# Sums of squares in four column groups, bonus sums in two float32r passes, block copies on GpSimd

## The chip, the cores and the metric

The kernel runs on one core of a Trainium2 chip. The metric is the time of one execution on the device, in microseconds (us). The core's engines work side by side, each through its own instructions in a fixed order: TensorE (PE; PEld is its loading of weights), VectorE (DVE), ScalarE (ACT), GpSimd (POOL) and SyncE (SP), which issues most of the DMAs.

## The reference

One inference step of a decoder with two layers, on a prompt of 256 tokens and eight tokens of eight running sequences, 264 columns in all. The model width is 1024, the inner width of the feed-forward blocks 2816. Each layer is a half-weighted SwiGLU, a mixer and another half-weighted SwiGLU, each behind an RMSNorm. The mixer of layer 0 is RWKV-7 time mixing with 16 heads of 64 channels, that of layer 1 is retention. The change lies in the first of these:

```python
r = xr @ wr;  k = xk @ wk;  v = xv @ wv
kk = hd(k * k_k)
kk = kk / jnp.maximum(jnp.sqrt(jnp.sum(kk * kk, axis=-1, keepdims=True)), 1e-12)
...
def step(S, inp):
    r_t, d_t, k_t, v_t, kk_t, a_t = inp
    sa = jnp.einsum('bhvk,bhk->bhv', S, -kk_t)
    S = (S * d_t[:, :, None, :] + sa[..., None] * (kk_t * a_t)[:, :, None, :]
         + v_t[..., None] * k_t[:, :, None, :])
    return S, jnp.einsum('bhvk,bhk->bhv', S, r_t)
...
y = y + jnp.sum(r_h * k_h * r_k.astype(f32), axis=-1, keepdims=True) * v_h
```

The sum of `kk * kk` over the 64 channels of each head is called the sums of squares below, and the sum in the last line the bonus.

## The kernel before

**Matrices.** The channels lie on the partitions in eight tiles of 128, so every activation is a 128x264 tile; a tile of 128 channels holds two heads, a pair. The weights come as 128x128 blocks, eight to a unit of 512 KB, which SyncE loads into one of three buffers (`raw`). Most products are done in float32r, in three passes over parts of the operands: ScalarE copies the unit to `hi` (`split`), VectorE subtracts it to give `lo`, and the matmuls are `ah,hi`, `al,hi` and `ah,lo`. The products for r, k and v in the time mixing (`xr,raw`, `xk,raw`, `xv,raw`) read the float32 block as it is, and float32 matmuls appear as two records each.

**Order.** The weight products are one main stream. Everything else of the layer is written as generators that stand beside it, each with a rank (`beside`). `weave` decides at each step of the stream which of them goes on, by modelled costs of every operation (`spent`) and by marks that one sets and another waits for (`mark`, and `yield` of a mark's name). From that program a scheduler fixes the order on every engine, in which its instructions then run one after another. So a change of any operation can move others that it doesn't touch.

**Time mixing.** These generators matter here.

- `lengths(g, sqs)`, for two groups of four pairs: matmuls with `hsel`, a 128x16 selection for each pair, add the squares of all four pairs into 16 rows of one PSUM tile; then square root, maximum and reciprocal give `rnr`.
- `stage(f)`, for each pair f: a matmul with `selT`, a 16x128 selection, brings the two rows of the pair back onto 128 partitions.
- `inverse`: a substitution of 32 steps on VectorE inverts the triangular blocks of all chunks; it ends with the mark `W0`. VectorE transposes the result (`AT`), ScalarE copies it into the blocks of `X` (L811 and on), and TensorE makes `tm,AT` and `V,AT` from it.
- `prep(f)`: the bonus operand `rc`, the product of r, k and `r_k`; for pairs 4 to 7 it begins behind the mark `W0`, for pairs 0 to 3 before it, but the last product, which gives `s_["bon"]`, comes behind `W0` for all.
- `heads2(p)`, for two pairs of tiles at a time: TensorE makes `KQ`, `PI,ka`, `cst,vt`, `VK,KQ`, `z,X` and others; ScalarE brings results from PSUM to SBUF (`bT`, `aT`, `vt`, `VK`, `z`). It ends with the bonus, a float32 matmul of `rc` with `bones`, a 128x128 constant with ones where two channels have the same head, shown as `ps<-rc,cst`.
- `decode`: the eight single tokens, with their states (`dS`, 512 KB each) loaded on GpSimd's queue and multiplied as `dS,kkr`.

The constants (`cst`, 128x1412) come by one DMA on ScalarE's queue, `selT` by another. A selection that is 32 wide, `rows64`, and its counterpart `back` are among the constants before too; the output norm uses them.

Of the kernel before, what the change touches and what calls it, by code (L numbers as in the profile page):

```python
# [11 lines left out]
F32R = mybir.dt.float32r  # L12
# [29 lines left out]
class Step:  # L42
# [158 lines left out]
    def mark(self, key):  # L201
        self.done[key] = self.now
# [242 lines left out]
class Rwkv(Step):  # L445
    def rw_consts(self, p):

        nc = self.nc
        c = p.tile([128, NCST], F32, name="cst")
        nc.scalar.dma_start(c, self.io["cst"])  # L450
        self.ident = c[:, CST["ident"]:CST["ident"] + 128]
        self.bones = c[:, CST["bones"]:CST["bones"] + 128]
        self.hsel = c[:, CST["hsel"]:CST["hsel"] + 128].rearrange("p (f h) -> p f h", f=KT)
        col = lambda k, n: c[:, CST[k]:CST[k] + n]
        self.m_ak, self.m_up = col("m_ak", 64), col("m_up", 64)
        self.m_kq = col("m_ak", 128)
        self.eye2 = col("eye2", 64)
        self.centre = col("centre", 128)
        self.rows64 = col("rows64", 64).rearrange("p (i m) -> p i m", i=2)
        self.back = col("back", 256).rearrange("p (i n) -> p i n", i=2)  # L460
        self.diag = col("diag", 4)
        self.pick = col("pick", 128).rearrange("p (e q n) -> p e q n", e=2, q=2)
        self.rst = col("rst", 256)

    def rwkv(self, gain):
# [6 lines left out]
        with ExitStack() as ctx:  # L472
# [19 lines left out]
                return h, l  # L492

            sh, xt = self.sh, self.xt

            hv = P1.tile([128, 4, KT], F32, name="hv")
            for i, k in enumerate(("w0", "a0", "ka")):
# [2 lines left out]
            epsg = P1.tile([128, 1], F32, name="epsg")  # L500
            nc.gpsimd.memset(epsg, 64e-5)
            big = lambda name: P.tile([128, 1024], F32, tag="big", name=name, bufs=3)
            selT = big("selT")[0:16].rearrange("p (f n) -> p f n", f=KT)
            nc.scalar.dma_start(selT, self.io["selT"])

            X = P1.tile([128, 32, 64], F32, name="X")
            for p0 in (32, 96):
# [200 lines left out]
            def lengths(g, sqs):  # L708
                yield f"k{g}"
                ssq = ps_()  # L710
                for j in range(4):
                    self.mm(ssq[0:16, 0:T], self.hsel[:, 4 * g + j, :], sqs[j], j == 0, j == 3)
                rn = tmp("mx")[0:16]
                self.act(rn, ssq[0:16, 0:T], AF.Sqrt)
                self.ts(rn, rn, 1e-12, None, ALU.max)
                rnr[g] = slot("rnr")[0:16]
                self.vec("reciprocal", rn, out=rnr[g])
                mark(f"rn{g}")
                yield
# [34 lines left out]
            def stage(f):  # L754
                yield f"rate{f}"
                yield f"rn{f // 4}"
                if f >= TU["SW"]:
                    yield "W0"
                if f >= 2:
                    yield f"stage{f - 2}"  # L760
                s_ = st[f]
                ta, cc, pp = s_["ta"], s_["cc"], s_["pp"]
                rb = ps_()[:, 0:T]
                self.mm(rb, selT[:, f, :], rnr[f // 4])
                kkn = tmp("kkn")
                self.stt(kkn, s_["k"], par("kk", f), rb)

                t_, kd = tmp("mx"), s_["k"]
                self.act(t_, ta, AF.Identity, scale=hv[:, 2, f:f + 1], bias=hv[:, 3, f:f + 1])
                self.tt(kd, t_, kd)  # L770
                u = ta
                self.stt(u, ta, 1.0, kkn, ALU.add, ALU.mult)
                gather(1, f, kkn[:, NP:T])
                nc.gpsimd.tensor_scalar(out=dq[:, 2, f, :], in0=u[:, NP:T], scalar1=-0.5, scalar2=None, op0=ALU.mult)
                gather(3, f, kd[:, NP:T])
                al, be, ka = (quarter(slot(n, 256)) for n in ("al", "be", "ka"))
                self.stt(al, r4(kkn), -1.0, pp[:, :, 0:64])
                self.stt(be, r4(u), 0.5, cc)
                self.tt(ka, r4(kd), cc)
                s_.update(rho=pp[:, :, 1:65], bon=kd, al=al, be=be, ka=ka)  # L780
                mark(f"stage{f}")
                yield

                pa = quarter(ps_()[:, 0:256])
                for c in range(NC):
                    for e0 in EH:
                        s, lo, hi = slice(e0, e0 + 64), slice(0, 32), slice(32, 64)
                        for r, i, j in ((lo, lo, 0), (hi, hi, 0), (hi, lo, 32)):
                            self.mm(pa[e0 + r.start:e0 + r.stop, c, j:j + 32], al[s, c, r], be[s, c, i])
                self.act(Ag[:, :, 4 * f:4 * f + 4].rearrange("p s n -> p n s"), pa[:, :, 0:32])  # L790
                for e0 in EH:
                    self.act(AT[e0 + 32:e0 + 64, 4 * f:4 * f + 4], pa[e0 + 32:e0 + 64, :, 32:64])
                mark(f"A{f}")
# [3 lines left out]
            def inverse():  # L797
                V, tm = (big(n).rearrange("p (a b) -> p a b", b=32) for n in ("V", "tm"))
                flat32 = lambda t: t.rearrange("p a b -> p (a b)")
                nc.gpsimd.memset(V, 0.0)  # L800
                nc.gpsimd.memset(flat32(V)[:, 0:1024:33], 1.0)
                for f in range(KT):
                    yield f"A{f}"
                self.turn(A3.rearrange("p r s -> p s r"), Ag)
                for m in range(31, 0, -1):
                    n = 32 - m
                    o = tm[:, 0:n, 0:m]
                    self.tt(o, V[:, m:32, m:m + 1].to_broadcast([128, n, m]),
                            A3[:, m:m + 1, 0:m].to_broadcast([128, n, m]))
                    self.tt(V[:, m:32, 0:m], V[:, m:32, 0:m], o, ALU.add)  # L810
                    if TU["INVY"] and m % TU["INVY"] == 0:  # L811
                        yield

                Xd = tm
                self.turn(Xd.rearrange("p n i -> p i n"), V)
                mark("W0")
                for e0 in EH:
                    self.turn(AT[e0:e0 + 32], Xd[e0:e0 + 32])
                for e0 in EH:
                    self.act(X[e0 + 32:e0 + 64, :, 32:64], Xd[e0 + 32:e0 + 64])  # L820
                    self.act(X[e0:e0 + 32, :, 0:32], Xd[e0:e0 + 32])
                yield
                for g in range(2):
                    py = ps_().rearrange("p (n s) -> p n s", n=16)
                    for n in range(16):
                        for e0 in EH:
                            hi = slice(e0 + 32, e0 + 64)
                            self.mm(py[e0:e0 + 32, n], AT[hi, 16 * g + n], Xd[hi, 16 * g + n])
                    for e0 in EH:
                        self.act(V[e0:e0 + 32, 16 * g:16 * g + 16], py[e0:e0 + 32])  # L830
                    yield
                for g in range(2):
                    px = ps_().rearrange("p (n s) -> p n s", n=16)
                    for n in range(16):
                        for e0 in EH:
                            lo = slice(e0, e0 + 32)
                            self.mm(px[lo, n], AT[lo, 16 * g + n], V[lo, 16 * g + n])
                    for e0 in EH:
                        self.act(X[e0:e0 + 32, 16 * g:16 * g + 16, 32:64], px[e0:e0 + 32])
                    mark(f"X{g}")  # L840
                    yield

            def prep(f):
# [8 lines left out]
                yield "W0"  # L852
                self.stt(rc, rc, par("rk", f), s_["bon"])
                s_["bon"] = rc
                mark(f"bon{f}")
                yield

# [10 lines left out]
            def heads2(p):  # L868
# [76 lines left out]
                for f, s_ in zip(fs, s2):  # L945
                    yield f"bon{f}"
                    pbo = ps_()[:, 0:T]
                    self.mm(pbo, self.bones, s_["bon"])
                    self.tt(s_["bon"], pbo, s_["vt"])
                yield  # L950
                pl = two()
# [193 lines left out]

CST = {}
_c = 0
for _k, _w in (("ident", 128), ("bones", 128), ("hsel", 128), ("m_ak", 64), ("m_up", 64), ("eye2", 64), ("centre", 128),
               ("rows64", 64), ("back", 256), ("diag", 4), ("pick", 128), ("rst", 256)):
    CST[_k] = _c  # L1150
    _c += _w
# [3 lines left out]
def consts():  # L1155
# [8 lines left out]

    put("ident", np.eye(128))
    put("bones", h[:, None] == h[None, :])
    hs = np.zeros((128, KT, 16))
    for f in range(KT):
        hs[p, f, 2 * f + h] = 1
    put("hsel", hs.reshape(128, 128))  # L1170

    put("m_ak", q[:, None] < s)
    put("m_up", q[:, None] <= s)
# [17 lines left out]
    r = np.ones((128, 4, 64))  # L1191
    r[:, :, 0] = 0
    put("rst", r.reshape(128, 256))
    sel = np.zeros((16, KT, 2, 64), np.float32)
    for f in range(KT):
        for e in range(2):
            sel[2 * f + e, f, e] = 1
    return c, sel.reshape(16, KT, 128)


def pack_wkv(s):
# [363 lines left out]

# [34 lines left out]
```

## Time and profile before

| | |
|---|---|
| median of three runs | 1288.61 us (1284.57 to 1290.11) |
| profiled execution | 1283.95 us, of which the span of the trace is 1282.2 |
| mean granted TensorE clock | 0.996 of full speed |
| TensorE busy | 1254.6 us, 98% |
| weight load, beside TensorE | 1184.4 us, 92% |
| VectorE, ScalarE, GpSimd busy | 849.4, 674.1, 68.8 us |

The span runs from the first to the last recorded instruction; the execution's time has 1.75 us more. Times inside the trace count from the start of the span. The time mixing lies between about 200 and 430 us and the retention's state sums at 869 us; feed-forward blocks stand around both. A row that covers several instructions has the start of the first and the time from there to the end of the last one; ends of matmuls are modelled.

### The profile page before, as it was taken

What the parts mean: (1) busy time and instruction counts of PE and PEld (TensorE: products, weight loads), DVE (VectorE), ACT (ScalarE), POOL (GpSimd) and SP (SyncE); (2) the same over time, 40 slices, a digit from 0 to 9 for tenths busy, and PEclk for the clock granted to TensorE, in tenths of its full rate; (3) what the DMA queues carried; (4) which work ended last, traced back from release to release, by engine and by line L of the source; (5) the groups of instructions that cost most, each with busy time, mean ns of one, the idle gap of its engine ahead of it and who ended that gap; (6) DMA issues with size and microseconds to landing.
All of it is one profiled execution on the core that took longest, in us unless ns stands there. A gap on an engine that the chain in (4) does not pass through costs nothing.

```text
span 1282.2 us, 29100 instructions
## 1 busy us (share of the span) xinstructions
PE 1254.6 (98%) x12194; PEld 1184.4 (92%) x12194; DVE 849.4 (66%) x1391; ACT 674.1 (53%) x1169; POOL 68.8 (5%) x175
## 2 busy tenths in 40 slices
PE   9999999999988999999999999999999999999996
PEld 9999998678777999999999999988888799999996
DVE  6766567589246877766566656677877865766554
ACT  7544442653444777754456454445665554544542
POOL 0000001131200000000000000011111100000000
PEclk9999999999999999999999999999999999999998
DMA  7655554333401566665557555679879655555562
GB/s 236 196 181 181 180 167 140 100 101 117 158 14 43 182 215 216 213 198 181 180 196 264 181 181 181 203 255 348 306 254 329 224 181 180 175 181 180 179 182 83
DMA packets 66755, 239.16 MB, mean 187 GB/s; under 512 B 7504, under 2 KB 8912, under 8 KB 66496
## 3 DMA queue, kind: packets, MB, share of 16 engines
q1 hardware_dynamic: 59472, 212.63, 51.8%
q0 software_dynamic: 6544, 23.40, 4.9%
q8 instruction: 95, 1.56, 0.5%
q10 hardware_dynamic: 608, 1.28, 0.3%
q14 instruction: 36, 0.29, 0.1%
HBM read 214.92 MB, written 22.35 MB: 185 GB/s over the span
## 4 chain that ended last, share of the span: by engine, by line
PE 87%; issue 5%; DMA 3%; DVE 2%; ACT 2%; SPq 0%; DVEq 0%; POOL 0%; ACTq 0%; POOLq 0%
PE ps L138 86%; DMA raw<-in_w 2%; PE ps L153 1%; DVE lo L105 1%; ACT hi L90 1%; DMA dS<-in_wkvt 1%; DMA Sd<-in_wkv 0%; DMA S<-in_ret 0%; ACT L90 0%; DMA out_swkv<-Sd 0%; DVE yl L105 0%; DVE xf L105 0%; DVE on L120 0%; DVE rs L126 0%; ACT sd L90 0%
## 5 line engine op out<-in xcount | busy, mean ns | idle before, releaser
L90 ACT ACTIVATE hi<-raw 128x1024 fp32r<-128x1024 f32 (+1 forms) x344 | 362.6, 1054 | 428.3 <-PE ps L138 210.4
L105 DVE TENSOR_TENSOR lo<-raw,hi 128x1024 fp32r<-128x1024 f32 (+1 forms) x344 | 418.5, 1217 | 229.6 <-ACT hi L90 228.1
L138 PE MATMUL ps<-ah,hi 128*128 128x264 f32 (+1 forms) x1824 | 522.0, 288 | 0.9 <-ACT ah L90 0.8
L138 PE MATMUL ps<-al,hi 128*128 128x264 f32 (+1 forms) x1824 | 515.8, 284 | 0.0
L138 PE MATMUL ps<-ah,lo 128*128 128x264 f32 (+1 forms) x1824 | 513.3, 284 | 0.1
L138 PEld LDWEIGHTS ps<-ah,hi 128*128 128x128 f32 x1824 | 342.0, 188 | 9.2 <-issue 7.4
L138 PEld LDWEIGHTS ps<-al,hi 128*128 128x128 f32 x1824 | 342.7, 188 | 4.1 <-issue 2.9
L138 PEld LDWEIGHTS ps<-ah,lo 128*128 128x128 f32 x1824 | 341.5, 188 | 0.5 <-DVE lo L105 0.3
L138 PE MATMUL ps<-hh,hi 128*128 128x264 f32 x832 | 237.1, 285 | 0.0
L138 PE MATMUL ps<-hl,hi 128*128 128x264 f32 x832 | 237.0, 285 | 0.0
L138 PE MATMUL ps<-hh,lo 128*128 128x264 f32 x832 | 236.8, 285 | 0.0
L138 PEld LDWEIGHTS ps<-hl,hi 128*128 128x128 f32 x832 | 156.8, 188 | 0.0
L138 PEld LDWEIGHTS ps<-hh,lo 128*128 128x128 f32 x832 | 156.7, 188 | 0.0
L138 PEld LDWEIGHTS ps<-hh,hi 128*128 128x128 f32 x832 | 156.4, 188 | 0.1
L105 DVE TENSOR_TENSOR h<-s,ps 128x264 f32<-128x264 f32 x88 | 37.0, 427 | 48.0 <-PE ps L138 46.6
L105 DVE TENSOR_TENSOR t<-ps,rs 128x264 f32<-128x264 f32 x88 | 37.2, 430 | 18.9 <-PE ps L138 18.8
L114 DVE SCALAR_TENSOR_TENSOR S<-ps,ks,S 128x512 f32<-128x512 f32 x64 | 45.0, 742 | 6.2 <-PE ps L138 6.2
L90 ACT ACTIVATE S<-S 128x1024 f32<-128x1024 f32 x32 | 33.7, 1056 | 16.1 <-DMA S<-in_ret 15.9
L90 ACT ACTIVATE hh<-h 128x264 fp32r<-128x264 f32 x88 | 35.3, 409 | 5.8 <-DVE h L105 5.5
L90 ACT ACTIVATE s<-t 128x264 f32<-128x264 f32 x88 | 35.3, 410 | 4.2 <-DVE t L105 4.1
L105 DVE TENSOR_TENSOR hl<-h,hh 128x264 fp32r<-128x264 f32 x88 | 37.0, 427 | 0.4
L90 ACT ACT_TABLE_LOAD x26 | 33.4, 1283 | 2.1 <-PEq L1580 1.7
(265 smaller groups left out, 1196.3 us busy)
## 6 DMA issues: line engine op xcount, KB each, us to landing
raw<-in_w SPq DMA_DIRECT2D x363, 512.0 KB, 3.7
S<-in_ret SPq DMA_DIRECT2D x32, 512.0 KB, 6.1
out_sret<-S POOLq DMA_DIRECT2D x32, 512.0 KB, 3.9
dS<-in_wkvt POOLq DMA_DIRECT2D x4, 512.0 KB, 5.4
Sd<-in_wkv SPq DMA_DIRECT2D x4, 512.0 KB, 5.7
out_swkv<-Sd POOLq DMA_DIRECT2D x4, 512.0 KB, 4.4
out_pret<-so POOLq DMA_DIRECT2D x8, 256.0 KB, 2.3
rcst<-in_rcst SPq DMA_DIRECT2D x1, 1100.0 KB, 6.2
```

The source lines that it names most:

```text
L90: ins = self.nc.scalar.activation(out=out, in_=in_, func=func, scale=scale, **kw)
L105: ins = self.nc.vector.tensor_tensor(out=out, in0=a, in1=b, op=op)
L114: ins = self.nc.vector.scalar_tensor_tensor(out=out, in0=a, scalar=s, in1=b, op0=op0, op1=op1)
L138: ins = self.nc.tensor.matmul(out=out, lhsT=lhsT, rhs=rhs, start=start, stop=stop)
L153: self.nc.tensor.transpose(out, in_, ident)
```

## The change

It has three parts. The sums of squares of four pairs go to four groups of 32 columns of the array, each a matmul of its own with `rows64`, so that square root, maximum and reciprocal work on 128 partitions and `stage` reads 32 rows of them with `back`; `rows64` carries a factor of 1/64, which the square root takes out by its scale. `hsel` and `selT` are no longer loaded, and the constants have 1284 columns. The bonus sums are two float32r matmuls: ScalarE copies `rc` to float32r and VectorE subtracts (`parts`, inside `prep` behind `W0`), and ScalarE copies `bones` to float32r (`bonesr`) at the start of the layer. The four copies into the blocks of `X` go from ScalarE to GpSimd.

```diff
@@ setup of the time mixing
-        self.hsel = c[:, CST["hsel"]:CST["hsel"] + 128].rearrange("p (f h) -> p f h", f=KT)
...
+            bonesr = P1.tile([128, 128], F32R, name="bonesr")
+            self.act(bonesr, self.bones)
...
-            selT = big("selT")[0:16].rearrange("p (f n) -> p f n", f=KT)
-            nc.scalar.dma_start(selT, self.io["selT"])
@@ lengths
                 for j in range(4):
-                    self.mm(ssq[0:16, 0:T], self.hsel[:, 4 * g + j, :], sqs[j], j == 0, j == 3)
-                rn = tmp("mx")[0:16]
-                self.act(rn, ssq[0:16, 0:T], AF.Sqrt)
+                    self.mm(ssq[32 * j:32 * j + 32, 0:T], self.rows64[:, 0], sqs[j], behind=j > 0)
+                rn = tmp("mx")
+                self.act(rn, ssq[:, 0:T], AF.Sqrt, scale=64.0)
                 self.ts(rn, rn, 1e-12, None, ALU.max)
-                rnr[g] = slot("rnr")[0:16]
+                rnr[g] = slot("rnr")
                 self.vec("reciprocal", rn, out=rnr[g])
@@ stage
-                self.mm(rb, selT[:, f, :], rnr[f // 4])
+                s = slice(32 * (f % 4), 32 * (f % 4) + 32)
+                self.mm(rb, self.back[s, 0], rnr[f // 4][s])
@@ inverse
-                    self.act(X[e0 + 32:e0 + 64, :, 32:64], Xd[e0 + 32:e0 + 64])
-                    self.act(X[e0:e0 + 32, :, 0:32], Xd[e0:e0 + 32])
+                    nc.gpsimd.tensor_copy(X[e0 + 32:e0 + 64, :, 32:64], Xd[e0 + 32:e0 + 64])
+                    nc.gpsimd.tensor_copy(X[e0:e0 + 32, :, 0:32], Xd[e0:e0 + 32])
@@ prep
                 yield "W0"
                 self.stt(rc, rc, par("rk", f), s_["bon"])
                 s_["bon"] = rc
+                s_["bp"] = parts(rc)
                 mark(f"bon{f}")
@@ heads2
                     yield f"bon{f}"
                     pbo = ps_()[:, 0:T]
-                    self.mm(pbo, self.bones, s_["bon"])
+                    for j in range(2):
+                        self.mm(pbo, bonesr, s_["bp"][j], j == 0, j == 1)
                     self.tt(s_["bon"], pbo, s_["vt"])
```

`behind` keeps a matmul in the program's order. Beside these lines the scheduler's order changes. On ScalarE, at the start of the layer, where `raw` is the first weight unit of the mixer and `cst` the constants:

```order
 L90 ACTIVATE ah<-x,par 128x264
 L90 ACTIVATE sq<-x 128x264
-L450 DMA cst<-in_cst 128x1412
-L504 DMA selT<-in_selT 16x1024
+L450 DMA cst<-in_cst 128x1284
+L90 ACTIVATE bonesr<-cst 128x128
 L90 ACTIVATE hi<-raw_2589 128x1024
 L90 ACTIVATE hi<-raw 128x1024
```

The copy of the ones block now stands between the issue of the constants' load and two splits of weights. On TensorE, the sums of squares of the second group, among products for r:

```order
 L138 MATMUL ps<-part,lo 128x264
-L138 MATMUL ps<-rnr,selT 128x264
-L138 MATMUL ps<-sq,cst 16x264
-L138 MATMUL ps<-xr,raw 128x264 x2
-L138 MATMUL ps<-sq,cst 16x264
+L138 MATMUL ps<-rnr,cst 128x264
+L138 MATMUL ps<-sq,cst 32x264
+L138 MATMUL ps<-xr,raw 128x264
+L138 MATMUL ps<-sq,cst 32x264
 L138 MATMUL ps<-part,hi 128x264 x2
 L138 MATMUL ps<-part,lo 128x264
```

Before and after, other products stand between these sums. On TensorE again, from the end of the substitution to the second block of `tm,AT` (`PI,ka`, `cst,vt` and `VK,KQ` are blocks of `heads2`, `xv,raw` the products for v):

```order
 L138 MATMUL ps<-cst,al 64x64 x24
-L138 MATMUL ps<-xv,raw 128x264 x25
-L138 MATMUL ps<-tm,AT 32x32 x32
-L138 MATMUL ps<-xv,raw 128x264
+L138 MATMUL ps<-xv,raw 128x264 x5
 L138 MATMUL ps<-PI,ka 64x64 x16
 L138 MATMUL ps<-cst,vt 64x64 x16
+L138 MATMUL ps<-xv,raw 128x264 x11
+L138 MATMUL ps<-VK,KQ 64x64 x16
+L138 MATMUL ps<-tm,AT 32x32 x32
+L138 MATMUL ps<-xv,raw 128x264 x29
+L138 MATMUL ps<-tm,AT 32x32 x32
```

One pair's blocks `PI,ka`, `cst,vt` and `VK,KQ` have moved ahead of the first `tm,AT`, and most of the products for v behind it. On ScalarE at the same place, where `tm` of the first removed row is `Xd`, the operand of the copies into `X`:

```order
 L90 ACTIVATE bT<-ps 128x256 x3
-L90 ACTIVATE X<-tm 32x32x32 x4
 L90 ACTIVATE vt<-ps 128x264
 L90 ACTIVATE aT<-ps 128x192 x4
-L90 ACTIVATE vt<-ps 128x264 x3
+L90 ACTIVATE part<-rc 128x264
+L90 ACTIVATE VK<-ps 128x512 x2
+L90 ACTIVATE part<-rc 128x264 x3
+L90 ACTIVATE vt<-ps 128x264
+L90 ACTIVATE z<-ps 128x256 x2
+L90 ACTIVATE part<-rc 128x264
 L90 ACTIVATE V<-ps 32x512 x2
```

The copies into `X` are gone from here, and the first bonus part stands ahead of the two copies of `VK`. The second block of `VK,KQ` now follows `V,AT` on TensorE, and the second block of `dS,kkr` stands behind eight more matmuls of the recurrence. GpSimd has the four copies into `X` behind its second `dq<-vt` and ahead of the loads of `dS`.

## Rows read from the trace of the kernel before

**Rows 1.** The page's first part: engine, busy us, share of the span, instructions.

```profile
PE 1254.6 (98%) x12194; PEld 1184.4 (92%) x12194; DVE 849.4 (66%) x1391; ACT 674.1 (53%) x1169; POOL 68.8 (5%) x175
```

**Rows 2.** Table by stage: span; busy PE, PEld, DVE, ACT, POOL; clock, DMA, GB/s.

```profile
340.00:430.00 90.00, 79.69 (x2075) 68.98 (x2066) 46.73 (x128) 39.73 (x103) 5.33 (x11) 0.98 0.21 65
```

**Rows 3.** Timeline of TensorE: start, length, engine, line, operation, tiles, count.

```profile
238.78 1.95 PE L138 MATMUL ps<-sq,cst 128*16 128x264 f32 x8
```

**Rows 4.** Timeline of TensorE, the retention's state sums.

```profile
869.03 1.92 PE L138 MATMUL ps<-S,qm 128*32 128x512 f32 x16
```

**Rows 5.** Timeline of TensorE, bonus sums between value products.

```profile
333.94 1.16 PE L138 MATMUL ps<-rc,cst 128*128 128x264 f32 x4
...
334.94 1.05 PE L138 MATMUL ps<-xv,raw 128*128 128x264 f32 x4
```

**Rows 6.** Table by stage, a stretch of float32r products (columns as above).

```profile
205.00:211.50 6.50, 6.50 (x52) 6.26 (x50) 4.47 (x4) 3.77 (x4) 0.00 (x0) 1.00 0.49 161
```

**Rows 7.** Instructions by line and form, 310 to 560 us: busy, mean ns; idle.

```profile
L90 ACT ACTIVATE part<-yl 128x264 fp32r<-128x264 f32 x8 | 3.3, 424 | 8.2 <-DVE yl L105 8.2
```

**Rows 8.** Timeline of ScalarE, start of the layer.

```profile
200.25 0.35 ACTq L450 DMA_DIRECT2D cst<-in_cst  x1
...
205.87 2.01 ACT L90 ACTIVATE hi<-raw 128x1024 fp32r<-128x1024 f32 x2 [4.79 <-PE ps L138]
```

**Rows 9.** DMA issues there: count, KB each, us from issue to landing.

```profile
cst<-in_cst ACTq DMA_DIRECT2D x1, 706.0 KB, 6.2
```

**Rows 10.** Timeline of VectorE, start of the layer.

```profile
209.35 1.80 DVE L126 RECIPROCAL rs<-sd 128x264 f32<-128x264 f32 x1
```

**Rows 11.** Timeline of TensorE, the first key products.

```profile
212.92 2.46 PE L138 MATMUL ps<-xk,raw 128*128 128x264 f32 x10 [1.37 <-issue]
```

**Rows 12.** Timeline of TensorE, around the end of the substitution.

```profile
305.37 11.39 PE L138 MATMUL ps<-xv,raw 128*128 128x264 f32 x50
...
316.69 1.20 PE L138 MATMUL ps<-tm,AT 32*32 32x32 f32 x64
...
318.47 1.00 PE L138 MATMUL ps<-PI,ka 64*64 64x64 f32 x30
...
320.85 0.71 PE L138 MATMUL ps<-xv,raw 128*128 128x264 f32 x2
```

**Rows 13.** Timeline of VectorE, behind the substitution.

```profile
316.21 1.71 DVE L114 SCALAR_TENSOR_TENSOR rc<-rc,par,k 128x264 f32<-128x264 f32 x4
```

**Rows 14.** Timeline of ScalarE, behind the substitution.

```profile
321.11 2.06 ACT L90 ACTIVATE VK<-ps 128x512 f32<-128x512 f32 x4
...
330.60 1.06 ACT L90 ACTIVATE hi<-raw 128x1024 fp32r<-128x1024 f32 x1 [1.20 <-DMA raw<-in_w]
```

**Rows 15.** The page's sixth part: DMA issues, KB each, median us to landing.

```profile
raw<-in_w SPq DMA_DIRECT2D x363, 512.0 KB, 3.7
...
dS<-in_wkvt POOLq DMA_DIRECT2D x4, 512.0 KB, 5.4
```

**Rows 16.** Table by stage, two stretches at the decode (columns as above).

```profile
343.00:346.20 3.20, 0.42 (x16) 0.18 (x6) 0.00 (x0) 0.00 (x0) 0.00 (x0) 1.00 0.11 44
...
346.30:349.70 3.40, 3.40 (x78) 2.72 (x80) 0.36 (x2) 0.61 (x2) 3.40 (x8) 0.51 0.39 75
```

**Rows 17.** Timeline of TensorE, the first decode products.

```profile
341.22 1.97 PE L138 MATMUL ps<-dS,kkr 64*32 64x64 f32 x123
```

**Rows 18.** Chain that ended last, 343 to 356 us: start, length, step.

```profile
347.66 6.75 DMA dS<-in_wkvt
```

**Rows 19.** Timeline of GpSimd, the memset of X.

```profile
200.52 1.93 POOL L508 MEMSET X<- 32x1024 f32 x2
```

**Rows 20.** Timeline of GpSimd, ahead of the substitution.

```profile
291.07 2.84 POOL L110 TENSOR_TENSOR PI<-cst,PL 128x256 f32<-128x256 f32 x4 [11.09 <-PE ps L138]
```

**Rows 21.** Timeline of VectorE, the same stretch.

```profile
290.64 0.40 DVE L105 TENSOR_TENSOR tm<-V,A 128x231 f32<-128x231 f32 x1
...
291.08 0.87 DVE L105 TENSOR_TENSOR V<-V,tm 128x231 f32<-128x231 f32 x1
```

More of the change, by code (lines that the diff above doesn't have):

```diff
@@ L1147 @@
 _c = 0
-for _k, _w in (("ident", 128), ("bones", 128), ("hsel", 128), ("m_ak", 64), ("m_up", 64), ("eye2", 64), ("centre", 128),
+for _k, _w in (("ident", 128), ("bones", 128), ("m_ak", 64), ("m_up", 64), ("eye2", 64), ("centre", 128),
                ("rows64", 64), ("back", 256), ("diag", 4), ("pick", 128), ("rst", 256)):
@@ L1166, in consts @@
     put("bones", h[:, None] == h[None, :])
[L1167 to L1170, printed above, removed]
     put("m_ak", q[:, None] < s)
@@ L1193, in consts @@
     put("rst", r.reshape(128, 256))
[L1194 to L1198, printed above, removed]
+    return c
 def pack_wkv(s):
@@ L1567 @@
     inp = {k: np.asarray(v) for k, v in inputs.items()}
-    cst, selT = consts()
+    cst = consts()
     rcst = ret_consts()
@@ L1571 @@
         x=pack_x(np.concatenate([inp["x_prompt"][0], inp["x_sample"][:, 0]], 0)),
-        par=pack_par(inp), cst=cst, selT=selT, rcst=rcst,
+        par=pack_par(inp), cst=cst, rcst=rcst,
         shift=pack_x(inp["state_rwkv_shift"][0]),
```

## Prediction

> **What bounds the kernel now.** I read the page's busy table first: TensorE is busy for 98% of the span [rows 1], so a microsecond of matmul removed is a microsecond won, and one in which TensorE stands still is lost. Next the table by stages: the token-mixing layer's tail, 340 to 430 us, is the place where TensorE is not full, 79.69 of 90 us [rows 2]. So the kernel has two currencies there: matmul time, and waiting in TensorE's fixed order. The change edits the first and, since the planner re-plans on the new costs, rearranges the second. A busy time counts the overlap of neighbours; I price a matmul by the distance from its start to the next start.
>
> **Sums of squares.** The first four matmuls (eight records, float32 takes two) are busy for 1.95 us [rows 3], 0.49 each. Afterwards they stand in four column groups. The nearest row is the retention's state sums, which stand so already, 32 columns a group: sixteen records over 512 columns in 1.92 us [rows 4], so 0.48 for four records side by side, 0.25 if 264 columns wide, and 0.5 for both halves. Gain 1.4 us; bounds 0 (they run in turn) and 1.5. The second four are not neighbours: the order shows other matmuls between them before and after. Gain 0. The selector matmuls keep their size and count: 0.
>
> **Bonus sums.** Two float32 ones take from 333.94 to 334.94 [rows 5], 0.50 each. Float32r: 205 to 211.5 us holds 52 records, nearly all of this kind, with no gap [rows 6], so a pass takes 0.125 and two 0.25. Gain 0.25 by eight, 2.0 us; bounds 1.0 (half lost when the array changes its shape) and 2.5. The price is eight ScalarE copies of 0.42 us (existing parts are the row) [rows 7] and as many VectorE subtractions; both engines have the time, so it is hidden where nothing stands behind them. But something does.
>
> **The copy of the ones block.** ScalarE now converts it ahead of the two weight splits that start at 205.87 [rows 8], and it needs the constants, which land 6.2 us after the issue at 200.25 [rows 8, 9]. That is 206.45, a little earlier with a tenth less data: say 206.2. With 0.3 us for the copy the splits start at 206.5, 0.65 later. VectorE's remainders of these splits stand ahead of its reciprocal, which started at 209.35 when the second of them was done, and on that reciprocal's chain waits TensorE's first key product: TensorE stood idle 1.37 us before 212.92 [rows 10, 11]. No slack, so +0.7; bounds 0.5 and 1.0.
>
> **The order behind the substitution (the largest term).** Before, TensorE went through 25 value products from 305.37 (0.453 each) [rows 12] while VectorE finished the inverse, and met the rest in time. Now 5 products, one pair's transposes and end-of-chunk products, and 11 products stand ahead of the first VK,KQ. The two pairs' blocks took 318.47 to 320.85 [rows 12], 1.19 a pair, so TensorE gets there at 305.37 + 16 x 0.453 + 1.19 = 313.8. VK comes from ScalarE, whose queue now has the first bonus part ahead of it. That part waits for VectorE's rc, which cannot start before both AT transposes end, at 316.21 [rows 13]. So: rc 0.43 (four took 1.71), part 0.42 [rows 7], two VK evictions at 0.52 (four took 2.06) [rows 14], and some 0.2 of hand-overs: 318.3. TensorE stands still for 4.5 us, I take 4.4, in place of none. Bounds: 3.9 (it may start on the first VK) and 7.5 (first rival).
>
> **The second pair.** All but three value products now lie ahead of the second tm,AT. The third weight split on ScalarE needs a weight buffer that the long run of 29 products frees, and a load takes 3.7 us to land, with such a split already seen waiting for its load [rows 14, 15]. From the end of that run TensorE has tm,AT 1.2 [rows 12], the pair's blocks 1.2, three products 1.36 and V,AT (as many as tm,AT) 1.2: 5.0 us. ScalarE has the load at 4.0 with its issue, the split 1.06, two VK 1.04 and 0.2 of hand-overs: 6.3. Wait 1.3, bounds 0 and 3. Then z,X needs the two X evictions queued behind VK and one vt, each some 0.5 again, with only the VK,KQ block to cover these 1.6 us, half as many matmuls as a pair's blocks, 0.6: wait 1.0. Before, eight value products stood there. Together +2.3.
>
> **The state loads of decode.** From 343 to 346.2 TensorE is busy for 0.42 of 3.20 us, a gap of 2.8 inside the first dS,kkr block that nothing in the profile releases; afterwards the granted clock is 0.51 from 346.3 to 349.7 [rows 16], the 1.2 GHz level: of these 3.4 us half, 1.7, is lost. The second dS load is issued when V,AT is done and lands 5.4 us later [rows 15]. Before, 334.94 to 341.22 covered it, seven value products among them [rows 5, 17]; without these 3.2 us, and with 0.5 of bonus sums, the cover is 3.6. With 0.3 to the issue the wait is 2.1. I take it to stand in the place of the gap, so -0.7; bounds -2.8 and +2.1 (both). Between the two dS,kkr blocks runs a chain that the change leaves: memset, issue, loads that end 6.75 us on [rows 18]. TensorE's work in it, and the half clock, fit under it before and after: 0.
>
> **The clock.** The new stall of 4.4 us is longer than the one ahead of the half clock in [rows 16], and behind it lie 29 products, with nothing to hide under: +1.7, bounds 0 and 3.4 (the dS wait as well).
>
> **X copies on GpSimd.** ScalarE loses four copies, which the added parts replace. GpSimd's copies cannot be seen; the nearest row, a memset of the same 32 x 1024 block, takes 0.97 (two in 1.93) [rows 19], the upper end is four times a 256-element GpSimd operation, 4 x 0.71 = 2.8. I take 1.0: X is needed some 25 us later, cost 0. While GpSimd read SBUF from 291.07 (2.84 us for four), VectorE's two-input operations rose from 0.40 to 0.87 [rows 20, 21]. By these rows the rc behind the substitution loses 0.3 to 0.5; I put it in the bound. The Trainium skill (SBUF — State Buffer, Who interferes with whom) says that a VectorE instruction with two SBUF inputs and a GpSimd instruction that reads SBUF exclude each other for a whole instruction; the rows agree in kind, and it is the first rival's rule.
>
> **Sum.** -1.4 - 2.0 + 0.7 + 4.4 + 2.3 - 0.7 + 1.7 = +5.0 us. The profiled execution took 1283.95 us (span 1282.2 and 1.75 around it), 4.7 below the median of the runs, 1288.61; so 1288.95 by its own time and 1293.6 on the scale of the median, on which the times below stand. That is 0.39%, under the 0.5% (6.4 us) that a measurement of this kernel can tell from no change: my forecast is the same time, on the slow side.
>
> **Rivals.**
> - GpSimd's copies hold up VectorE (slower). Place: rc at 316.21. If a copy takes 2.8 us, the second runs from 316.5 to 319.3 and the first rc waits for its end, 3.1 us, then VK: the stall is 7.5. Total +8.1, 1296.7. It decides from 1.4 us of extra wait, thus copies of some 2 us. For it: [rows 20]; against it: [rows 19]. Chance 0.17. By the skill's rule above, rc waits for the copy in flight, whatever its length: the stall is then what the copy has left to run.
> - The weight load lands late (slower). If it takes the 6.2 us that the constants took [rows 9], the second pair waits 2.5 longer: +7.5, 1296.1. Chance 0.14; against it speaks the 3.7 median [rows 15].
> - The waits are worth less (same). If the clock holds and neither the gap nor a dS wait is left: 5.0 - 1.7 - 2.1 = +1.2, 1289.8. Chance 0.17.
> - The change doesn't do what it says: the column groups run in turn. +6.4, 1295.0. Or the gap stands beside the dS wait, +7.8, 1296.4. Chance 0.08, most of it slower.
> - Only the savings arrive (faster at best): -3.4 and no new wait gives 1285.2, still within 0.5%; a gain beyond that needs the gap of 2.8 and its half clock gone as well, 1280.7. For it: nothing in the orders. Chance 0.07, of it 0.04 beyond.
>
> **Numbers.** The forecast has 0.37, its own range 1290 to 1297. Slower than 1295.0 are the first rival, the second, 0.06 of the fourth, and by its upper edge 0.01 of the forecast: 0.38. Faster 0.04, and the rest, 0.58, the same. The range, 1286.5 to 1300, goes from just above the savings' case to the first rival with a second clock dip (1296.7 + 1.7) and some 1.5 us of the runs' scatter.
>
> **What would show it.** The first sq block 0.5 us long; eight float32r pairs some 0.25 us apart. TensorE idle about 4 us ahead of the first VK,KQ, released by ScalarE's VK, with part<-rc just ahead of it; a second wait of 1 to 2 us at the next VK,KQ; waits on X; a dS wait; the key product 0.7 us later behind bonesr. A granted clock of half after the first stall. I am wrong if VK,KQ starts without a wait, if GpSimd's X copies are far from 1 us, or if the layer ends earlier than 430 us less the savings.

## The result and the profile after

The changed kernel takes 1299.39 us (median of four runs, 1296.44 to 1300.92) against 1288.88 us: ratio 1.0081, 95% interval 1.006 to 1.0102, 10.4 us slower. A second measurement gave 1297.56 against 1287.48 us, ratio 1.0085 (1.0071 to 1.0098). The forecast was 1293.6 us, the same time on the slow side. The loss was foreseen in kind and place, and came out twice as large: by its interval it is a loss of 0.6 to 1.0%, more than the 0.5% up to which the prediction called a time the same.

The page's busy table of the changed kernel, which answers to [rows 1]: TensorE is busy for 7.5 us more, in a span that is 15.7 us longer.

```profile
span 1297.9 us, 29120 instructions
PE 1262.1 (97%) x12194; PEld 1193.0 (92%) x12194; DVE 854.3 (66%) x1399; ACT 673.7 (52%) x1174; POOL 73.4 (6%) x179
```

The 15.7 us aren't the effect. Part of them lies outside the layer, and this execution has two stretches of half clock (365.0 to 368.3 and 426.4 to 429.8 us) that a second profiled execution, with a span of 1293.1 us, hasn't. From VectorE's first `xk` to the first sum of `x` behind the layer it is 209.0 us before, 221.6 in the first and 218.3 in the second profile. The layer's loss is 9.3 us by the second. It lies between `xk` and the first copy of `G` on ScalarE (+12.8 and +12.2 us); behind that the changed kernel is no slower. (Before, the pause of 2.78 us at 345.98 us and the half clock of [rows 16] lie behind that copy, in the changed kernel the pauses begin ahead of it.)

TensorE's timeline of the changed kernel from the end of the substitution (start, length, then the instructions, in brackets the idle time ahead of them and who ended it), which answers to [rows 12]:

```profile
310.90 5.16 PE L138 MATMUL ps<-xv,raw 128*128 128x264 f32 x22
320.27 0.33 PE L138 MATMUL ps<-VK,KQ 64*64 64x64 f32 x4 [4.21 <-ACT VK L90]
320.76 1.12 PE L138 MATMUL ps<-VK,KQ 64*64 64x64 f32 x28 [0.16 <-ACT VK L90]
321.81 1.92 PE L138 MATMUL ps<-tm,AT 32*32 32x32 f32 x64
323.65 15.00 PE L138 MATMUL ps<-xv,raw 128*128 128x264 f32 x58
338.59 1.20 PE L138 MATMUL ps<-tm,AT 32*32 32x32 f32 x64
...
344.24 0.33 PE L138 MATMUL ps<-VK,KQ 64*64 64x64 f32 x4 [0.70 <-ACT VK L90]
...
346.17 0.63 PE L138 MATMUL ps<-z,X 64*64 64x64 f32 x27 [0.32 <-ACT X L90]
```

The stall of 4.21 us stands where the order had put it. Who VK waits for is seen in the timelines of ScalarE, VectorE and GpSimd at the same place:

```profile
306.80 1.25 ACT L90 ACTIVATE aT<-ps 128x192 f32<-128x192 f32 x4 [0.46 <-PE ps L138]
319.31 0.42 ACT L90 ACTIVATE part<-rc 128x264 fp32r<-128x264 f32 x1 [11.26 <-DVE rc L114]
319.64 1.07 ACT L90 ACTIVATE VK<-ps 128x512 f32<-128x512 f32 x2
```

```profile
315.71 2.50 DVE L132 STREAM_TRANSPOSE AT<-tm 32x1024 f32<-32x1024 f32 x2
318.24 1.04 DVE L114 SCALAR_TENSOR_TENSOR rc<-rc,par,k 128x264 f32<-128x264 f32 x1
...
320.39 0.48 DVE L114 SCALAR_TENSOR_TENSOR rc<-rc,par,k 128x264 f32<-128x264 f32 x1
```

```profile
317.96 1.04 POOL L821 COPY X<-tm 32x1024 f32<-32x1024 f32 x1
319.04 1.14 POOL L822 COPY X<-tm 32x1024 f32<-32x1024 f32 x1
```

ScalarE stands still for 11.26 us with the first part at its head, waiting for VectorE's `rc`, while the operand of VK lies ready in PSUM since the blocks `cst,vt` ended, at about 311 us. The first `rc` takes 1.04 us beside a copy into X, a later one 0.48.

The table by stages for the stall, the 6.8 us behind it, and the stretch after that (busy us of PE, PEld, DVE, ACT and POOL with their counts, then the granted clock, DMA share and GB/s); the last line is the same place in the second profile:

```profile
316.10:320.27 4.17, 0.00 (x0) 0.00 (x0) 3.62 (x4) 0.96 (x3) 3.94 (x4) 1.00 0.48 126
320.60:327.40 6.80, 6.64 (x102) 5.63 (x102) 4.84 (x13) 3.37 (x10) 0.45 (x1) 0.50 0.01 2
327.50:338.50 11.00, 11.00 (x51) 9.18 (x49) 2.59 (x6) 3.46 (x8) 0.45 (x1) 1.00 0.40 112
```

```profile
319.50:326.20 6.70, 6.70 (x101) 5.69 (x102) 4.74 (x13) 3.33 (x9) 0.44 (x1) 0.50 0.01 2
```

Behind the stall the granted clock is 0.50, the 1.2 GHz level, for 6.8 us, in both profiles. Half of that, 3.4 us, is lost, since TensorE is busy for nearly all of it.

At the decode there are again pauses that no engine ends. These answer to the gap in [rows 16]; the second of them, of 1.64 us, has the clock at 1.00 behind it:

```profile
351.66 0.38 PE L138 MATMUL ps<-M,WT 64*64 64x64 f32 x3 [1.79 <-issue]
...
359.21 0.31 PE L138 MATMUL ps<-dS,kkr 64*32 64x64 f32 x7 [1.64 <-issue]
...
363.30 0.46 PE L138 MATMUL ps<-pp,ka 64*64 64x64 f32 x16 [1.65 <-issue]
```

At the start of the layer, the sums of squares take 0.65 us in place of 1.95 [rows 3], but two waits for other engines' work now stand ahead of the substitution:

```profile
240.50 0.65 PE L138 MATMUL ps<-sq,cst 128*32 128x264 f32 x8
...
263.58 0.73 PE L138 MATMUL ps<-be,al 64*32 64x32 f32 x48 [0.31 <-DVE be L114]
...
271.72 0.73 PE L138 MATMUL ps<-be,al 64*32 64x32 f32 x48 [0.56 <-ACT dq L90]
```

And the copy of the ones block, on ScalarE:

```profile
207.34 0.31 ACT L90 ACTIVATE bonesr<-cst 128x128 fp32r<-128x128 f32 x1 [4.60 <-DMA cst<-in_cst]
207.55 1.99 ACT L90 ACTIVATE hi<-raw 128x1024 fp32r<-128x1024 f32 x2
```

The split that follows starts 1.68 us later than before (205.87), and VectorE's first `xk` is 1.66 us later too. That shift is there from the first 35 us of the run on. The copy costs nothing here: before, the split had waited 4.79 us for TensorE to leave its buffer [rows 8], and the copy lies inside that wait. It only just fits: with the bonus sums alone, where the constants are the longer ones, they land later, and the first `xk` is 12.53 us behind their issue in place of 12.07.

### The profile page after: what moved, and what is told of

Read it like the earlier page. It is cut to its first block, busy times and chain, and to the rows that moved or that the text cites. A ratio compares the mean times of both kernels' runs of the same rounds, so it can differ in the third digit from the quotient of the medians.

```text
span 1297.9 us, 29120 instructions
## 1 busy us (share of the span) xinstructions
PE 1262.1 (97%) x12194; PEld 1193.0 (92%) x12194; DVE 854.3 (66%) x1399; ACT 673.7 (52%) x1174; POOL 73.4 (6%) x179
## 4 chain that ended last, share of the span: by engine, by line
PE 87%; issue 5%; DVE 5%; ACT 2%; DMA 1%; DVEq 0%; SPq 0%; POOLq 0%; ACTq 0%
PE ps L138 86%; PE ps L153 1%; DVE V L105 1%; DVE tm L105 1%; DMA raw<-in_w 1%; DMA Sd<-in_wkv 0%; ACT hi L90 0%; ACT L90 0%; DMA out_swkv<-Sd 0%; DVE yl L105 0%; DVE AT L132 0%; DVE KQ L105 0%; DVE lo L105 0%; DVE xf L105 0%; ACT VK L90 0%
## 5 line engine op out<-in xcount | busy, mean ns | idle before, releaser
L138 PE MATMUL ps<-part,hi 128*128 128x264 f32 (+1 forms) x176 | 35.1, 311 | 0.1
```

Source lines behind the costliest of these rows:

```text
L138: ins = self.nc.tensor.matmul(out=out, lhsT=lhsT, rhs=rhs, start=start, stop=stop)
```

## The experiments

Each run is compared with the kernel before on the same chip. The theory: TensorE waits in its fixed order for results that stand in ScalarE's queue behind work that itself waits (a bonus part for VectorE, a weight split for its load), and a long wait costs again by the clock. Rivals were the edits' own prices: the passes, the column groups, GpSimd's copies.

### One part at a time

**Sums of squares alone** (the hunks on `hsel`, `selT`, `lengths` and `stage`; the rest of before).

> Only the sums of squares are changed; bonus in float32 and X copies on ScalarE as before. The order behind the substitution stays that of before (25 value products ahead of the first tm,AT). Theory (the loss is the order behind the substitution): the first sums take 0.65 us in place of 1.95, and the planner gives most of this back ahead of the substitution, so between -1.3 and +0.5 us against the kernel before: the same time. Rival (the column groups themselves, with their wider reciprocal rows, delay the start of the substitution and so the layer): +1.5 us or more, with the substitution starting later than before.

Measured: ratio 0.9991 (0.9978 to 1.0004), 1.2 us faster by it, but not clear of no change. As the theory has it. The substitution starts 0.3 us later, counted from the first `xk`, with the two waits shown above at the same places. The rival's +1.5 us in the time is out: the interval ends at +0.5.

**Bonus sums alone** (`bonesr`, `parts(rc)` in `prep`, two passes).

> Only the bonus sums are changed (float32r, parts made behind the substitution); sums of squares and X copies as before. TensorE still meets the first tm,AT after 25 value products, but 22 more of them are packed ahead of the second. Theory: no stall ahead of the first tm,AT; a wait of 1 to 4 us at VK,KQ and z,X of the second pair, because ScalarE has eight parts and weight splits queued ahead of VK; a bonus sum 0.35 us in place of 0.50, 1.2 us in all; so +1 to +4 us. Rival (the passes alone decide): -1.2 us.

Measured: ratio 1.0098 (1.0079 to 1.0117), 12.6 us slower, as slow as the whole change and three times my upper bound. The eight bonus sums themselves are cheaper; the wait at the second pair is larger than I thought. ScalarE, then TensorE, then the table by stages:

```profile
338.02 1.06 ACT L90 ACTIVATE hi<-raw 128x1024 fp32r<-128x1024 f32 x1 [2.69 <-DMA raw<-in_w]
338.98 1.07 ACT L90 ACTIVATE VK<-ps 128x512 f32<-128x512 f32 x2
```

```profile
339.62 1.61 PE L138 MATMUL ps<-VK,KQ 64*64 64x64 f32 x32 [3.87 <-ACT VK L90]
```

```profile
339.10:352.60 13.50, 12.15 (x352) 11.10 (x356) 3.24 (x7) 6.54 (x14) 1.74 (x3) 0.50 0.41 142
```

The second VK stands behind a weight split that waits for its load: the mechanism of the prediction's second pair, here with a stall of 3.87 us and two more waits of 1.33 and 0.69 us beside it. It is not the second rival's slow load: this one was issued at 334.26 us and landed 3.8 us later. Behind the stall lie 13.5 us at half clock, some 6 us more. Twenty-two products packed ahead of the second `tm,AT` leave nothing to cover these waits.

**X copies alone on GpSimd** (the two lines in `inverse`).

> Only the X copies go to GpSimd; sums of squares and bonus as before. The planner now puts one pair's VK,KQ and only 16 value products ahead of the first tm,AT. Theory: no part stands ahead of VK on ScalarE, so VK,KQ runs at once, but tm,AT then waits for the transposes: TensorE reaches it at 305.4 + 16 x 0.453 + 1.19 + 0.6 = 314.4 us in the time of the trace of before, and the transposes end at 316.2, a stall of 1.8 us and, if the clock falls behind it, 1.7 to 3.4 more: +2 to +5 us. Rival (the copies only hold up VectorE, the order costs nothing): rc at 1.0 us in place of 0.5, less than +0.6 us.

Measured: ratio 1.0047 (1.0032 to 1.0063), 6.1 us slower, a little above the theory's range, and the rival's 0.6 us is out. But the place is not the one I gave. `tm,AT` ran without a wait, so my stall at the transposes was wrong. The time went at 346 us instead:

```profile
353.00 1.06 ACT L90 ACTIVATE hi<-raw 128x1024 fp32r<-128x1024 f32 x1 [5.58 <-DMA raw<-in_w]
353.96 0.20 ACT L90 ACTIVATE yd<-ps 128x64 f32<-128x64 f32 x1
```

```profile
354.22 0.48 PE L138 MATMUL ps<-cst,yd 128*64 128x64 f32 x4 [8.64 <-ACT yd L90]
```

A copy of 0.20 us, `yd`, is queued behind a split that waits 5.58 us for its weights, and TensorE stands still for 8.64 us; from 349.7 to 359.8 us the granted clock is 0.50. Why does a copy that moved off ScalarE do this? By its code the planner charges ScalarE's copies to ScalarE and these copies on GpSimd to nobody, so 4 us come free in its plan. Its new order has one pair's blocks further ahead and value products as late as 363.75 us, and the load for that split is issued only at 348.70 us and takes 4.3. That the missing charge makes this order was not tried by an experiment.

### The place of the parts

**Both savings, parts made late, X copies on ScalarE.** The parts move from `prep` (first hunk) to `heads2` (second).

```diff
                 s_["bon"] = rc
-                s_["bp"] = parts(rc)
                 mark(f"bon{f}")
...
                     yield f"bon{f}"
+                    s_["bp"] = parts(s_["bon"])
                     pbo = ps_()[:, 0:T]
```

> Column groups and float32r bonus sums, but the parts are made in heads2 just ahead of the bonus sum, and the X copies stay on ScalarE. The order behind the substitution is then that of before (25 products, tm,AT, single products between the pairs' blocks). Theory: both savings and no new wait there: -1.3 - 1.2, with up to 1.5 us given back ahead of the substitution: -2.5 to -0.5 us. Rival (the savings are lost in the dependent chain in any order): 0 to +3 us.

Measured: ratio 0.9982 (0.9971 to 0.9993), 2.3 us faster than before, the fastest kernel of the study. The passes and the parts are those of the bonus sums alone, and the times are 15 us apart; the column groups account for 1.2 of these, and what else differs is the place at which the parts are made, with the order that follows from it. On ScalarE nothing waits ahead of VK any more:

```profile
321.87 2.06 ACT L90 ACTIVATE VK<-ps 128x512 f32<-128x512 f32 x4
...
329.81 0.73 ACT L90 ACTIVATE part<-rc 128x264 fp32r<-128x264 f32 x2
```

**The same with the X copies on GpSimd.**

> All three parts of the change, but the bonus parts are made in heads2 just ahead of the bonus sum. The order behind the substitution is nearly that with the X copies alone on GpSimd (16 products, VK,KQ, then tm,AT with three products between). Theory: the two losses are separate, so this has the loss of the X copies alone (+6.8 us) less the savings of 2.4 us: +3 to +6 us. Rival (only the two together make the loss): -1 to +1 us.

Measured: ratio 1.0054 (1.0036 to 1.0072), 7.0 us slower. The rival is out: late parts don't cure the loss of the X copies. That the savings of 2.4 us would come off it isn't seen; the time is that of the X copies alone, within the intervals. The trace has the same kind of stall: a copy of `G` behind a split that waits 5.88 us for its load holds TensorE up for 3.51 us at 350.07.

**The changed kernel with VK ahead of the parts.** `heads2` sets a mark once VK of the first pair is evicted, and `prep` waits for it.

```diff
                 s_["bon"] = rc
+                yield "VK0"
                 s_["bp"] = parts(rc)
...
                     self.act(VK[i], pv[i])
+                if p == 0:
+                    mark("VK0")
```

> The changed kernel, but no part is made until VK of the first pair has been evicted; VK then stands ahead of the parts on ScalarE, and the eight parts stand ahead of z, V and the second VK. TensorE has 16 value products ahead of VK,KQ as in the changed kernel, but 10 in place of 29 between the two tm,AT. Theory (the place of the parts in ScalarE's queue decides where TensorE waits): no wait for VK at the first VK,KQ, 1 to 2 us at tm,AT for the transposes, then a wait of about 2 us for V behind the parts, and less half clock: +2 to +7 us. Rival (the loss stems from having fewer products ahead of the substitution's end, whatever ScalarE does): still +10 us.

Measured: ratio 1.0007 (0.9992 to 1.0021), 0.9 us slower (by its interval −1.0 to +2.7): by its middle better than the theory's range, and 9.5 us better than the changed kernel. Nine tenths of the loss hang on that place in the queue and on the packing that follows from it (ten products in place of 29 between the two `tm,AT`); this run changes both and doesn't part them. The wait for the transposes that I expected didn't come. TensorE and VectorE:

```profile
315.16 0.69 PE L138 MATMUL ps<-VK,KQ 64*64 64x64 f32 x32
315.79 1.20 PE L138 MATMUL ps<-tm,AT 32*32 32x32 f32 x64
```

```profile
314.87 2.50 DVE L132 STREAM_TRANSPOSE AT<-tm 32x1024 f32<-32x1024 f32 x2
317.41 2.22 DVE L114 SCALAR_TENSOR_TENSOR rc<-rc,par,k 128x264 f32<-128x264 f32 x2
```

`tm,AT` starts at 315.79, 1.6 us ahead of the end of the two transposes: it doesn't wait for both. Nor does TensorE wait for V; a wait of 1.21 us for `z`, which also stands behind the parts, came in its place.

**The same edit without GpSimd's copies**, on both savings.

> Column groups and float32r bonus sums with X copies on ScalarE; parts are made as in the changed kernel, but only once VK of the first pair has been evicted. The planner then has 25 products ahead of the first tm,AT and spreads single products between the blocks, as before the change; on ScalarE seven parts still stand ahead of the first VK copies' successors and of V. Theory (the long run of products and ScalarE's queue make the loss, not the splitting itself): one or two waits of about 1 us for VK and V, less the savings of 2.4 us: -1.5 to +1 us. Rival (parts in prep delay the layer wherever they stand): +5 us or more.

Measured: ratio 1.0018 (1.0008 to 1.0027), 2.3 us slower, a little above the theory's range and well under the rival. Parts made early cost 4.6 us more than parts made late (−2.3). ScalarE's rows show seven parts and two copies of V ahead of VK; TensorE waits only 0.16 us for it and later 0.93 us for WT. In the two profiles the layer is 3.0 us longer than with the late parts; it has half clock for 10.2 us (6.8 of them behind two pauses of 1.7 us that no engine ends) where the late parts have 3.4, and half of the difference, 3.4 us, is lost. How much of that is the order's and how much chance, one profile of each doesn't tell.

```profile
321.01 1.36 ACT L90 ACTIVATE part<-rc 128x264 fp32r<-128x264 f32 x4
322.28 1.17 ACT L90 ACTIVATE V<-ps 32x512 f32<-32x512 f32 x2
323.48 1.05 ACT L90 ACTIVATE part<-rc 128x264 fp32r<-128x264 f32 x3
324.55 1.09 ACT L90 ACTIVATE VK<-ps 128x512 f32<-128x512 f32 x2
```

### What the stall costs

**Work in place of the stall.** Fifteen float32 products whose results nobody reads, ahead of the first VK,KQ.

```diff
+                if p == 0:
+                    fill = ps_()[:, 0:T]
+                    for j in range(15):
+                        nc.tensor.matmul(out=fill, lhsT=self.bones, rhs=s2[1]["vt"], start=j == 0, stop=j == 14)
                 pz = two()
```

> The changed kernel with fifteen extra float32 products of 264 columns (results unused) ahead of the first VK,KQ, so that TensorE works while it waits for VK. The planner puts 10 value products in front of it in place of 16; the other six, 2.7 us, come later. Theory (the stall of 4.2 us costs twice, since the granted clock falls to half behind it for 6.8 us): VK,KQ starts at the same time as in the changed kernel, no half clock around 320 to 327 us, 3.4 us won, 2.7 lost: about +9.7 us against the kernel before. Rival (the clock falls there for another reason): the half clock stays, +13 us.

Measured: ratio 1.0066 (1.005 to 1.0083), 8.5 us slower than before, so by the middles some 2 us faster than the changed kernel (the intervals overlap), with 6.8 us of useless matmuls in it and 2.7 us of products moved behind them. TensorE's timeline and the table by stages:

```profile
312.99 6.84 PE L930 MATMUL ps<-vt,cst 128*128 128x264 f32 x30
320.03 0.33 PE L138 MATMUL ps<-VK,KQ 64*64 64x64 f32 x4 [0.21 <-ACT VK L90]
...
323.80 14.51 PE L138 MATMUL ps<-xv,raw 128*128 128x264 f32 x64
...
352.79 0.59 PE L138 MATMUL ps<-bT,WT 64*64 64x64 f32 x11 [3.88 <-issue]
```

```profile
320.60:327.40 6.80, 6.80 (x114) 5.73 (x115) 4.71 (x13) 2.07 (x6) 0.45 (x1) 1.00 0.06 17
```

VK,KQ starts when it did, the clock from 320.6 to 327.4 us is 1.00 in place of 0.50, and 32 products take 14.51 us where 29 took 15.00. So this half clock belongs to the stall. A pause of 3.88 us came up later, with 6.8 us at half clock around it.

**Without the copies into X.** This run leaves the diagonal blocks of X zero; the orders on TensorE and ScalarE are those of the changed kernel.

> The changed kernel without the four copies into X (X is set to zero at the start, so the products with X are left without their diagonal blocks); the orders on TensorE and ScalarE are those of the changed kernel. Theory: rc takes 0.5 us in place of 1.04 and the first stall 3.6 in place of 4.2, the rest stays: +9.5 to +10.4 us against the kernel before. Rival (GpSimd's copies hold up VectorE and so cause the loss): +7 us or less.

Measured: ratio 1.0068 (1.0046 to 1.0089), 8.8 us slower, under the theory's range by its middle, over the rival's; the interval, 5.9 to 11.5 us, reaches into both, and the trace decides. VectorE and TensorE:

```profile
317.81 0.49 DVE L114 SCALAR_TENSOR_TENSOR rc<-rc,par,k 128x264 f32<-128x264 f32 x1
```

```profile
319.30 1.61 PE L138 MATMUL ps<-VK,KQ 64*64 64x64 f32 x32 [3.64 <-ACT VK L90]
...
322.69 15.85 PE L138 MATMUL ps<-xv,raw 128*128 128x264 f32 x58
```

```profile
317.80:328.00 10.20, 8.69 (x108) 7.19 (x109) 6.86 (x17) 5.49 (x14) 0.19 (x1) 0.50 0.09 35
```

Without a copy beside it `rc` takes 0.49 us, and the stall is 0.57 us shorter. That is what GpSimd's reading adds in this kernel; a stall of 3.64 us stays, so the loss isn't made by it. What the shorter stall gained went to the clock: it is at half for 10.2 us in place of 6.8, and the 29 products take 15.85 us in place of 15.00. The Trainium skill (SBUF — State Buffer, Who interferes with whom) has a VectorE instruction with two inputs in SBUF and a GpSimd instruction that reads SBUF shut each other out for a whole instruction; the rows agree in kind, with 0.55 us between an `rc` beside a copy and one without.

**The changed kernel again**, for a second profile.

> The changed kernel once more, for a second profile. Theory (order and queues, fixed by the program, make the loss): the waits for VK of 4.2 and 0.7 us, the half clock from 320 to 327 us and the pauses between 349 and 364 us stand at the same places within 1 us, and the time is +9 to +12 us against the kernel before. Rival (a part of the loss in the first profile is chance): a stall or a half clock inside the layer is gone or elsewhere.

Measured: ratio 1.0085 (1.0071 to 1.0098), 10.9 us slower. The first stall is 4.18 us, the second wait 0.51, the half clock lies at the same place, the pause at `M,WT` is 1.65 and that at `dS,kkr` 1.64. These are the order's. The third pause is 1.10 us in place of 1.65, and the half clock at 365 and 426 us is not there: for these 6.8 us of half clock, 3.4 us of time, the rival is right.

## Why the prediction was right and where it was short

| step, as the prediction put it | predicted us | measured us |
|---|---|---|
| sums of squares | −1.4 | −1.3 at their place, +0.3 by the start of the substitution |
| bonus sums | −2.0 | −1.1 and −1.3 (eight sums 4.62, now 3.54 and 3.30) |
| copy of the ones block | +0.7 | 0 |
| order behind the substitution | +4.4 | +4.4 and +4.3 (4.21 and 0.16; 4.18 and 0.15) |
| second pair | +2.3 | +1.2 and +1.0 (0.70, 0.16, 0.32; 0.51, 0.16, 0.32) |
| state loads of decode | −0.7 | +1.0 and 0 (pauses 5.4 and 4.4, before 4.4) |
| clock | +1.7 | +3.4 |
| sum | +5.0 | +9.2 and +7.7, with +0.3 for the sums of squares |

Where the measured column has two values, they are of the first and the second profile of the changed kernel; the layer is 12.6 and 9.3 us longer in them. The rows leave out what lies behind 364 us. Pauses there are 0.9 and 1.6 us longer than before, and the first profile alone has 6.8 us of half clock, 3.4 us of time. With these the rows come to 13.5 and 9.3 us, so both are accounted for to about 1 us.

**Right.** The largest term: the part ahead of VK, at the place and of the size given, which the run with VK ahead took away. The copies into X at 1.03 us, `rc` held up by half a microsecond as in the bounds, the second pair in its place, at half the size, and the half clock behind the stall. The first rival's mechanism is there, but copies of 1.03 us are far from the 2 us from which it decides. The second rival's slow load did not come: the load that the second pair's first split waited for landed 3.6 us behind its issue.

**Short by its sizes.** The clock was costed at half of what it took: I took one stretch of 3.4 us as in [rows 16], and it was 6.8 us. The state loads were wrong in kind: a wait for `dS` was to take the place of the gap. No wait for `dS` came, and the gap came back as three pauses, with as much half clock as before. The sums of squares were costed by their matmuls alone: the 1.3 us arrive, but new waits of 1.0 us stand behind them, and the substitution starts 0.3 us later, as the run with them alone shows. The copy of the ones block was costed on the splits' start time without asking what the splits waited for; the row that I cited had the answer, 4.79 us on TensorE. Two bonus sums that stand together save 0.31 us for both, and most of the others 0.2 each, not 0.25. These errors mostly point the same way, hence 5 us became 9 to 13.

**Luck.** The time, 1299.39 us, is above the forecast's own 1290 to 1297 and 0.6 us below the upper edge of the range. That edge was drawn for the first rival with a second fall of the clock; the time came near it without that rival's long copies, by half clock and pauses that the sum had too small.

**Not seen.** That the bonus edit alone costs as much as all three. I had added the terms of one order; in another order (the bonus alone) the same parts put the second VK behind a waiting split.

## What to carry to other kernels

An engine's queue runs in order, so a short copy that others wait for must not stand behind an instruction that itself waits for a third engine or a load: here a part of 0.42 us and a split of 1.06 us each held TensorE up for 4 to 9 us. Make such helper values just ahead of their use, not as soon as they can be made: with the copies into X left on ScalarE, +1.0% (bonus sums alone) became −0.2%, of which the column groups are 0.1%. With these copies on GpSimd it was not enough (+0.5%). And when a planner orders the program, read its new order before the edit is judged, since an operation moved to an engine that it doesn't charge for frees time only in the plan.

## What the hardware showed

The half clock behind a stall was not of one length: 3.4 us behind the pause of 2.78 us in the kernel before and behind one of 1.65 in the second profile, 6.8 us behind the stall of 4.2, 10.2 us with the stall of 3.64 in the run without the copies into X, 13.5 us with a stall of 3.87 and short waits within it. With work put in the stall's place it did not come.

The pauses that nothing in the profile releases stand close behind packets on the instruction queue, of which the trace of the changed kernel has 96 for TensorE's 24,388 matmuls and weight loads, one for some 254. In the DMA table of the changed kernel, each of the three windows that begin ahead of the pauses at 351.66, 359.21 and 363.30 us has one packet on the instruction queue (queue, kind: packets, MB, share); the windows here are 348.6 to 349.9, 356.5 to 357.6 and 360.4 to 361.6 us:

```profile
q8 instruction: 1, 0.02, 7.9%
...
q8 instruction: 1, 0.02, 7.6%
...
q8 instruction: 1, 0.02, 6.7%
```

By the trace's records they land at 350.35, 357.92 and 361.80 us, and TensorE goes on 1.31, 1.29 and 1.50 us later. The same holds for every pause behind the substitution that no engine ends, five more in this trace and five in that of the kernel before, the gap of 2.78 us among them: TensorE goes on 1.3 to 1.5 us behind such a landing. Most landings in the layer, 22 of 30 in this trace, have no pause behind them. The Trainium skill (Runtime: NRT & Kernel Launch, Instruction fetch mechanics) has each engine fetch its instructions in blocks by a DMA queue of its own, and calls that mostly hidden; by these rows it isn't hidden here, if the pauses are the fetches'. That the fetch is what TensorE waits for was not tried by an experiment.
